# Gate reads a group ahead, four U tiles before the first V product, and the low part of g behind that of V, in a decoder layer's PEER experts

## The chip, the cores and the metric

The kernel runs on one core of a Trainium2 chip. The metric is device time of one launch in microseconds, the median of the runs shown. Five engines work side by side and meet at semaphores: PE (matmuls), DVE (vector), ACT (scalar), POOL (GpSimd, here the row gathers) and SP, which issues loads and stores. All transfers go through 16 DMA engines.

## What is computed

One decoder layer, 512 tokens of width 1024: two token mixers and an output projection, then a PEER layer, which is what the change is about. Each token picks 8 x 16 of 16384 experts by product keys. An expert is a row u and a row v of 1024 numbers:

```python
def peer_ffn(h, w_q, sub_keys, u_tab, v_tab):
    ...
    top_s, pos = lax.top_k(cand, PEER_TOPK)
    e_idx = jnp.take_along_axis(cand_idx, pos, axis=-1)
    gw = jax.nn.softmax(top_s, axis=-1).astype(h.dtype)
    ...
    ue = u_tab[ec]
    ve = v_tab[ec]
    act = jax.nn.gelu(jnp.einsum('td,thkd->thk', hc, ue), approximate=False)
    return jnp.einsum('thk,thkd->td', gc * act, ve)
```

## The kernel before

The kernel computes PEER for the first 384 tokens (TD) densely, without gathers: over all 16384 experts, in 128 tiles of 128 experts. For each tile there is a U product (rows of u times h, then gelu, called act) and a V product, which adds g = gate x act, times rows of v, into six accumulators va. The gate matrix is zero where a token did not pick an expert. It is built while the U tiles run (`w_chunk`, `w_mm`), 24 chunks of 16 tokens, each written to the scratch tensor `wd` in memory by an ACT-issued store. The last 128 tokens go another way: POOL gathers the 256 rows of u and v that each of them picked (`ldg`, one column of indices at a time), and DVE multiplies and adds them (`gather_step`, lines 1171 and 1179).

Numbers are split into a high and a low part for the matmuls: ACT casts the high one (`uhi`, `vhi`, `gshi`, line 122), DVE subtracts to get the low one (`ulo`, `vlo`, `gslo`, line 114). So a U tile is 24 matmuls of 384 columns (lines 1070 to 1072) and a V product is 18 of 512 (lines 1295 to 1297).

There are three stretches. First the loop with `work(...)`: 88 U tiles beside the building of the gate matrix and the first 60 gather steps. The first 8 activations stay on chip (`RING`), the other 80 are spilled to `spill`. Then the V loop: for each of the first 40 products one of the 40 U tiles that are left runs too, with about three gather steps. Then V alone, 88 products, with about one gather step each. `order` says which tile a product takes: 0 to 7, then the tiles whose activation was never spilled, then the spilled ones from 8 on.

`v_prep(n)` readies product n: it loads the gate group of 8 tiles (`wt`, 1.57 MB in pieces of 512 bytes, two buffers), for spilled tiles a group of 4 activations (`sp`, 0.79 MB, two buffers), and the rows of V (`ld`, 0.52 MB; four buffers, shared with the rows of U). It then makes g, its split and that of V. `vhi` and `vlo` have two buffers, so ACT may cast V of product n only when PE is through with n - 2. DVE's order is that of the code; the order on PE, ACT and SP is made by a scheduler when the program is built. The part of `v_prep` that matters:

```python
        g = vp.tile([P, TD], F32, name="g", bufs=2)
        tt(g.rearrange("p (c t) -> p c t", t=16), wt[:, :, i % 8, :], ac.rearrange("p (c t) -> p c t", t=16), mult)
        gs = split(vp, vp, g, [P, TD], "gs", bufs=KL)
        ...
            v = split(vp, vp, vst[n], [P, D], "v", bufs=2)
```

Of the kernel before, what the change touches and what calls it, by code (L numbers as in the profile page):

```python
# [9 lines left out]
F32 = mybir.dt.float32  # L10
# [10 lines left out]
P = 128  # L21
# [8 lines left out]
TD = 384  # L30
# [78 lines left out]
def layer(ctx: ExitStack, tc: tile.TileContext, a, out):  # L109
    nc = tc.nc  # L110
    mult, add, sub = ALU.mult, ALU.add, ALU.subtract

    def tt(o, i0, i1, op):
        return nc.vector.tensor_tensor(out=o, in0=i0, in1=i1, op=op)  # L114

    def act(o, i, f, **k):
        return nc.scalar.activation(o, i, f, **k)  # L117

    def split(pool_hi, pool_lo, src, shape, tag, bufs=1):
        hi = pool_hi.tile(shape, F32R, name=tag + "hi", bufs=bufs)  # L120
        lo = pool_lo.tile(shape, F32R, name=tag + "lo", bufs=bufs)
        nc.scalar.copy(hi, src)  # L122
        tt(lo, src, hi.bitcast(F32), sub)
        return hi, lo
# [4 lines left out]
    wd = dram.tile([P, TD // 16, NTILE, 16], F32, name="wd")  # L129
# [15 lines left out]
    with ExitStack() as pre:  # L145
# [630 lines left out]
        for i in range(N + 2):  # L776
            n, pr = i // 4, i % 4
# [57 lines left out]
        rt = ctx.enter_context(ExitStack())  # L835
# [212 lines left out]
    spill = dram.tile([P, NTILE, TD], F32, name="spill")  # L1048
    RING = 8

    def ld():
        return ua.tile([P, D], F32, name="ld", bufs=4)

    ust, usp, ue, PU, UB = [], [], [], 2, 3

    def u_split(i):
        if i >= NTILE or i < len(usp):
            return
        while len(ust) < min(i + PU + 1, NTILE):
            ust.append(ld())  # L1060
            nc.sync.dma_start(ust[-1], a["uT"][len(ust) - 1].rearrange("p d e -> p (d e)"))
        src = ust[i].rearrange("p (d e) -> p d e", d=ND)
        usp.append(split(ua, ua, src, [P, ND, P], "u", bufs=UB))

    def u_mm(i, spilled=False):
        u_split(i)
        hi, lo = usp[i]
        ps = psU.tile([P, TD], F32, name="u")
        for d in range(ND):
            nc.tensor.matmul(ps, hi[:, d, :], h2hi[:, d, :TD], start=d == 0, stop=False)  # L1070
            nc.tensor.matmul(ps, hi[:, d, :], h2lo[:, d, :TD], start=False, stop=False)  # L1071
            nc.tensor.matmul(ps, lo[:, d, :], h2hi[:, d, :TD], start=False, stop=d == ND - 1)  # L1072
        ue.append((i, ps, spilled))

    def u_evac():
        if not ue:
            return
        i, ps, spilled = ue.pop(0)
        if spilled:
            ac = up_.tile([P, TD], F32, name="actw", bufs=2)  # L1080
            act(ac, ps, AF.Gelu)
            nc.scalar.dma_start(spill[:, i, :], ac)
        else:
            ac = up_.tile([P, TD], F32, name="act", bufs=RING)
            act(ac, ps, AF.Gelu)
            acts[i] = ac
# [23 lines left out]
    pend = []  # L1110
# [71 lines left out]
    items = [(c, f, 0.0) for c, f in dq]  # L1182
# [10 lines left out]
    r, bud, lead, GR, gcr = 0, 0.0, 3.7, 0.75, 0.0  # L1193

    def work(lim):
        nonlocal bud
        while items and bud > lim:
            c, f, p = items.pop(0)
            f()
            bud += p - c  # L1200

    for i in range(UB - 1):
        u_split(i)
    while items or pend or r % 8:
        bud += lead - 1.14
        todo, pend[:] = list(pend), []
        work(2.0)
        u_split(r + UB - 1)
        u_evac()
        work(0.0)  # L1210
        if gather_on:
            gcr += GR
            while gcr >= 1.0:
                gcr -= 1.0
                gq.pop(0)()
                bud -= 1.2
        for f in todo:
            f()
        u_mm(r, r >= RING)
        r += 1  # L1220
    u_evac()
    rt.close()
    order = list(range(min(RING, r))) + list(range(r, NTILE)) + list(range(RING, r))

    vp = ctx.enter_context(tc.tile_pool(name="vpool", bufs=1, side="left"))
    psV = ctx.enter_context(tc.tile_pool(name="psV", bufs=1, space=PSUM))
    vac = [[psV.tile([P, 512], F32, name=f"va{t}{k}") for k in range(2)] for t in range(ND_T)]
    xos = {}
# [20 lines left out]
            x1_load(t)  # L1249
        final(ND_T)  # L1250

    wts, sps, vst = {}, {}, []
    KL = 4

    vsp = {}

    def v_prep(n):
        if n >= NTILE:
            return
        i = order[n]  # L1260
        if i // 8 not in wts:
            wts.clear()
            wts[i // 8] = vp.tile([P, TD // 16, 8, 16], F32, name="wt", bufs=2)
            nc.sync.dma_start(wts[i // 8], wd[:, :, i // 8 * 8:i // 8 * 8 + 8, :])
        wt = wts[i // 8]
        if i in acts:
            ac = acts.pop(i)
        else:
            if i // 4 not in sps:
                sps.clear()  # L1270
                sps[i // 4] = vp.tile([P, 4, TD], F32, name="sp", bufs=2)
                nc.sync.dma_start(sps[i // 4], spill[:, i // 4 * 4:i // 4 * 4 + 4, :])
            ac = sps[i // 4][:, i % 4, :]
        while len(vst) < min(n + 2, NTILE):
            m = order[len(vst)]
            vst.append(ld())
            nc.sync.dma_start(vst[-1], a["vn"][m * P:(m + 1) * P, :])
        g = vp.tile([P, TD], F32, name="g", bufs=2)
        tt(g.rearrange("p (c t) -> p c t", t=16), wt[:, :, i % 8, :], ac.rearrange("p (c t) -> p c t", t=16), mult)
        gs = split(vp, vp, g, [P, TD], "gs", bufs=KL)  # L1280
        if n >= NTILE - KL + 2:
            v = split(ua, ua, vst[n].rearrange("p (d e) -> p d e", d=ND), [P, ND, P], "u", bufs=UB)
            v = tuple(z.rearrange("p d e -> p (d e)") for z in v)
        else:
            v = split(vp, vp, vst[n], [P, D], "v", bufs=2)
        vsp[n] = gs + v

    def v_mm(n, ts=range(ND_T), kk=range(2)):
# [13 lines left out]
    rho = (sum(base) + 1.46 * len(gq)) / (0.98 * 3.9 * (NTILE + nu))  # L1302
    dma_t, pe_t, nxt = 0.0, 0.0, r
    v_prep(0)
    for n in range(NTILE - KL):
        v_prep(n + 1)
        if nxt < NTILE:
            u_split(nxt + UB - 1)
            u_mm(nxt)
            nxt += 1  # L1310
            pe_t += 3.9
        dma_t += base[n]
        while todo and dma_t < rho * pe_t:
            c, f = todo.pop(0)
            f()
            dma_t += c
        v_mm(n)
        u_evac()
        pe_t += 3.9
    for n in range(NTILE - KL, NTILE):  # L1320
        v_prep(n + 1)
# [27 lines left out]
```

## Time and profile before

| what | value |
|---|---|
| runs | 1631.23, 1631.67, 1636.91 us; median 1631.67 |
| the profiled execution | 1632.98 us, its span 1631.2 us |
| busy: PE, PE's weight loads, DVE, ACT, POOL | 96%, 84%, 80%, 46%, 20% of the span |
| moved by DMA | 413.16 MB |
| V products and the gathers beside them, 915 to 1598 us | DMA engines 0.94 to 0.96 busy, 326 to 338 GB/s |

Busy time of PE is not PE at its peak, since matmuls are pipelined: a matmul is shown as busy from its issue to its end, and the next one begins before that. Where PE is held up must be read from the starts of its matmuls. In a timeline, the number in brackets at a row's end is the time for which the engine stood idle before it, and who ended that wait.

### The profile page before, as it was taken

To read this page: it belongs to the slowest core of one execution; us is meant where nothing else is said; L and a number is where in the kernel's file an instruction comes from. 1 tells how busy PE (TensorE), PEld (TensorE's weight loads), DVE (VectorE), ACT (ScalarE), POOL (GpSimd) and SP (SyncE) were. 2 spreads that over 40 slices of the span, in tenths; PEclk is the share of its full clock that TensorE was granted. 3 is DMA by queue.
4 is the path that set the end of the run, shared out by engine and by line. 5 is a ranking of instruction groups with operands and counts; after the bars stand their busy time and mean duration, and the time that the engine had idled before them with its cause. 6 is when DMAs were issued, how large, how long until landed. Compare 5 with 4: busy or idle time off the path is not lost.

```text
span 1631.2 us, 24125 instructions
## 1 busy us (share of the span) xinstructions
PE 1564.7 (96%) x9033; PEld 1362.5 (84%) x9033; DVE 1297.7 (80%) x2590; ACT 757.8 (46%) x1234; POOL 330.9 (20%) x266
## 2 busy tenths in 40 slices
PE   6999998999999999999999799999999999999998
PEld 3779766898889999999999699998988777877877
DVE  4698667578989999988888587787878777777777
ACT  4345568634335544877877323332332333333332
POOL 0000000000002232222222153454444312222210
PEclk9999999999999999999999899999999999999999
DMA  8443332334016787988888998999999999999993
GB/s 308 154 156 118 116 143 78 120 139 156 1 39 240 260 275 255 324 312 317 311 313 292 310 350 315 334 331 322 333 323 344 315 310 319 347 355 327 326 319 125
DMA packets 153358, 413.16 MB, mean 253 GB/s; under 512 B 12940, under 2 KB 72588, under 8 KB 144152
## 3 DMA queue, kind: packets, MB, share of 16 engines
q1 hardware_dynamic: 100816, 234.37, 41.8%
q0 software_dynamic: 36864, 134.23, 23.1%
q10 hardware_dynamic: 15560, 43.01, 7.0%
q8 instruction: 71, 1.16, 0.3%
q14 instruction: 47, 0.39, 0.1%
HBM read 365.89 MB, written 45.09 MB: 252 GB/s over the span
## 4 chain that ended last, share of the span: by engine, by line
PE 65%; DVE 15%; DMA 13%; ACT 4%; issue 2%; SPq 0%; ACTq 0%; DVEq 0%
DMA ld<-in_vn_dram 9%; PE u L1070 7%; PE u L1071 7%; PE u L1072 7%; PE va L1296 6%; PE va L1297 5%; PE va L1295 5%; DVE ldg L1171 3%; DVE acc L1179 3%; DVE ulo L114 2%; DVE vlo L114 2%; ACT vhi L122 2%; PE mm L1026 2%; PE mm L1025 2%; PE mm L1027 2%
## 5 line engine op out<-in xcount | busy, mean ns | idle before, releaser
L1070 PE MATMUL u<-h2hi,uhi 128*128 128x384 f32 x1024 | 350.8, 343 | 4.2 <-ACT act L117 3.9
L1072 PE MATMUL u<-h2hi,ulo 128*128 128x384 f32 x1024 | 346.8, 339 | 4.3 <-DVE ulo L114 4.3
L1071 PE MATMUL u<-h2lo,uhi 128*128 128x384 f32 x1024 | 348.8, 341 | 0.0
L1163 POOL DMA_INDIRECT ldg<-in_un_dram,e_i x128 | 163.6, 1278 | 884.4 <-DVE cand L114 505.5
L1295 PE MATMUL va<-vhi,gshi 128*128 128x512 f32 x756 | 295.3, 393 | 16.9 <-ACT gshi L122 15.2
L1296 PE MATMUL va<-vlo,gshi 128*128 128x512 f32 x756 | 298.2, 394 | 8.0 <-DVE vlo L114 7.9
L1297 PE MATMUL va<-vhi,gslo 128*128 128x512 f32 x756 | 296.4, 392 | 0.0
L1163 POOL DMA_INDIRECT ldg<-in_vn_dram,e_i x128 | 165.1, 1290 | 350.8 <-DVE acc L1179 311.6
L122 ACT CAST vhi<-ld 128x1024 fp32r<-128x1024 f32 x126 | 132.3, 1051 | 204.6 <-PE va L1297 87.7
L1070 PEld LDWEIGHTS u<-h2hi,uhi 128*128 128x128 f32 x1024 | 194.6, 190 | 7.3 <-ACT act L117 5.1
L122 ACT CAST uhi<-ld 128x1024 fp32r<-128x1024 f32 x130 | 137.6, 1059 | 131.4 <-PE u L1071 75.8
L1072 PEld LDWEIGHTS u<-h2hi,ulo 128*128 128x128 f32 x1024 | 194.3, 190 | 5.0 <-DVE ulo L114 4.9
L1071 PEld LDWEIGHTS u<-h2lo,uhi 128*128 128x128 f32 x1024 | 194.7, 190 | 1.4
L1295 PEld LDWEIGHTS va<-vhi,gshi 128*128 128x128 f32 x756 | 142.8, 189 | 48.9 <-ACT gshi L122 17.5
L1296 PEld LDWEIGHTS va<-vlo,gshi 128*128 128x128 f32 x756 | 142.7, 189 | 41.7 <-DVE vlo L114 13.4
L114 DVE TENSOR_TENSOR ulo<-ld,uhi 128x1024 fp32r<-128x1024 f32 x130 | 158.5, 1220 | 17.6 <-ACT uhi L122 16.1
L114 DVE TENSOR_TENSOR vlo<-ld,vhi 128x1024 fp32r<-128x1024 f32 x126 | 153.8, 1221 | 22.7 <-ACT vhi L122 22.7
L114 DVE TENSOR_TENSOR gslo<-g,gshi 128x384 fp32r<-128x384 f32 x128 | 71.5, 559 | 121.3 <-ACT gshi L122 121.3
L1297 PEld LDWEIGHTS va<-vhi,gslo 128*128 128x128 f32 x756 | 142.7, 189 | 29.3
L1179 DVE SCALAR_TENSOR_TENSOR acc<-ldg,actg,acc 128x1024 f32<-128x1024 f32 x127 | 162.5, 1280 | 0.0
L122 ACT CAST gshi<-g 128x384 fp32r<-128x384 f32 x128 | 65.3, 510 | 196.6 <-DVE g L114 196.3
L1171 DVE SCALAR_TENSOR_TENSOR ldg<-ldg,h2n 128x1024 f32<-128x1024 f32 x128 | 155.9, 1218 | 0.0
(317 smaller groups left out, 2533.1 us busy)
## 6 DMA issues: line engine op xcount, KB each, us to landing
ld<-in_uT_dram SPq DMA_DIRECT2D x128, 512.0 KB
ld<-in_vn_dram SPq DMA_DIRECT2D x128, 512.0 KB
wst<-in_wada_dram SPq DMA_DIRECT2D x24, 1024.0 KB
wd<-wb ACTq DMA_DIRECT2D x24, 1024.0 KB
wt<-wd SPq DMA_DIRECT2D x16, 1536.0 KB
spill<-actw ACTq DMA_DIRECT2D x80, 192.0 KB
sp<-spill SPq DMA_DIRECT2D x20, 768.0 KB
wst<-in_win_dram SPq DMA_DIRECT2D x9, 1024.0 KB
```

The lines of the kernel that those rows point to most:

```text
L114: return nc.vector.tensor_tensor(out=o, in0=i0, in1=i1, op=op)
L122: nc.scalar.copy(hi, src)
L1025: nc.tensor.matmul(ps2[c][:, ms_], hi[:, d, wc], h2hi[:, d, ms_], start=d == 0, stop=False)
L1070: nc.tensor.matmul(ps, hi[:, d, :], h2hi[:, d, :TD], start=d == 0, stop=False)
L1071: nc.tensor.matmul(ps, hi[:, d, :], h2lo[:, d, :TD], start=False, stop=False)
L1072: nc.tensor.matmul(ps, lo[:, d, :], h2hi[:, d, :TD], start=False, stop=d == ND - 1)
L1163: nc.gpsimd.indirect_dma_start(out=gst[-1], out_offset=None, in_=a["un" if kind == "u" else "vn"], in_offset=bass.IndirectOffsetOnAxis(ap= ...
L1171: nc.vector.scalar_tensor_tensor(g, g, 1.0, h2n, op0=mult, op1=mult, accum_out=actg[:, k:k + 1])
L1179: nc.vector.scalar_tensor_tensor(acc, g, actg[:, k:k + 1], acc, op0=mult, op1=add)
L1295: nc.tensor.matmul(vac[t][k], ghi[:, ts_], vhi[:, ks], start=f, stop=False)
L1296: nc.tensor.matmul(vac[t][k], ghi[:, ts_], vlo[:, ks], start=False, stop=False)
L1297: nc.tensor.matmul(vac[t][k], glo[:, ts_], vhi[:, ks], start=False, stop=l)
```

## The change

There are three edits and one that follows from them. The first loop no longer runs on to a multiple of 8 tiles; a second loop runs four more U tiles (and on to a multiple of 4) without gather steps, asks for the first gate group in it, and spills these tiles too. That makes 92 tiles ahead of the V loop, 84 of them spilled. `group_load` keeps the last two groups; `v_prep` asks for the next gate group when it is at the third or seventh tile of a group of 8, and for the next spilled group when it is at the first of a group of 4 and the next one is no more than 12 products away. And the split of g stands behind that of V.

```diff
-    while items or pend or r % 8:
+    while items or pend:
...
+    rt.close()
+
+    vp = ctx.enter_context(tc.tile_pool(name="vpool", bufs=1, side="left"))
+    wts, sps, vst = {}, {}, []
+
+    def group_load(held, k, name, src):
+        if k not in held:
+            held[k] = vp.tile(list(src.shape), F32, name=name, bufs=2)
+            nc.sync.dma_start(held[k], src)
+            for j in list(held)[:-2]:
+                del held[j]
+
+    def w_load(k):
+        group_load(wts, k, "wt", wd[:, :, k * 8:k * 8 + 8, :])
+
+    def s_load(k):
+        group_load(sps, k, "sp", spill[:, k * 4:k * 4 + 4, :])
+
+    last_r = r + 4
+    while r < last_r or r % 4:
+        u_split(r + UB - 1)
+        if r == last_r - 4 + 1:
+            w_load(0)
+        u_evac()
+        u_mm(r, r >= RING)
+        r += 1
     u_evac()
-    rt.close()
...
+    def follow(ks):
+        out = [k for k, j in zip(ks, [None] + ks[:-1]) if k != j]
+        return out
+
+    wseq = follow([i // 8 for i in order])
+    sseq = follow([i // 4 for i in order if RING <= i < r])
...
     def v_prep(n):
...
-        if i // 8 not in wts:
-            wts.clear()
-            wts[i // 8] = vp.tile([P, TD // 16, 8, 16], F32, name="wt", bufs=2)
-            nc.sync.dma_start(wts[i // 8], wd[:, :, i // 8 * 8:i // 8 * 8 + 8, :])
+        if n == 0 or i // 8 != order[n - 1] // 8:
+            w_load(i // 8)
+            wseq.pop(0)
...
-            if i // 4 not in sps:
-                sps.clear()
-                sps[i // 4] = vp.tile([P, 4, TD], F32, name="sp", bufs=2)
-                nc.sync.dma_start(sps[i // 4], spill[:, i // 4 * 4:i // 4 * 4 + 4, :])
+            if i % 4 == 0:
+                s_load(i // 4)
+                sseq.pop(0)
...
+        if i % 4 == 2 and wseq:
+            w_load(wseq[0])
+        if i % 4 == 0 and sseq and n + 12 >= order.index(sseq[0] * 4):
+            s_load(sseq[0])
         g = vp.tile([P, TD], F32, name="g", bufs=2)
         tt(g.rearrange("p (c t) -> p c t", t=16), wt[:, :, i % 8, :], ac.rearrange("p (c t) -> p c t", t=16), mult)
-        gs = split(vp, vp, g, [P, TD], "gs", bufs=KL)
...
             v = split(vp, vp, vst[n], [P, D], "v", bufs=2)
+        gs = split(vp, vp, g, [P, TD], "gs", bufs=KL)
```

SP's order where the first loop ends, before (`ld<-in_uT` and `ld<-in_vn` are rows of U and V, `wt` is a gate group, `sp` a spilled group):

```order
L1061 DMA ld<-in_uT_dram 128x1024 x86
L1277 DMA ld<-in_vn_dram 128x1024 x2
L1264 DMA wt<-wd 128x24x128 x2
L1277 DMA ld<-in_vn_dram 128x1024
L1272 DMA sp<-spill 128x1536
```

and in the changed kernel:

```order
L1061 DMA ld<-in_uT_dram 128x1024 x89
L1229 DMA wt<-wd 128x24x128
L1061 DMA ld<-in_uT_dram 128x1024
L1304 DMA ld<-in_vn_dram 128x1024
L1229 DMA wt<-wd 128x24x128
L1304 DMA ld<-in_vn_dram 128x1024 x2
L1229 DMA sp<-spill 128x1536 x2
```

The two loads of V rows that stood ahead of the first gate group stand behind it now, the second of them behind the second gate group too, and the last U load as well.

DVE's order in one round while U and V alternate, before:

```order
L114 TENSOR_TENSOR g<-wt,act 128x384
L114 TENSOR_TENSOR gslo<-g,gshi 128x384
L114 TENSOR_TENSOR vlo<-ld,vhi 128x1024
L114 TENSOR_TENSOR ulo<-ld,uhi 128x1024
L1171 SCALAR_TENSOR_TENSOR ldg,actg<-ldg,h2n 128x1024
```

and in the changed kernel:

```order
L114 TENSOR_TENSOR g<-wt,act 128x384
L114 TENSOR_TENSOR vlo<-ld,vhi 128x1024
L114 TENSOR_TENSOR gslo<-g,gshi 128x384
L114 TENSOR_TENSOR ulo<-ld,uhi 128x1024
L1171 SCALAR_TENSOR_TENSOR ldg,actg<-ldg,h2n 128x1024
```

Only the low parts of g and V have changed places; on ACT the cast of g still stands ahead of that of V in most of these rounds.

SP's order where V stands alone, before:

```order
L1277 DMA ld<-in_vn_dram 128x1024 x4
L1272 DMA sp<-spill 128x1536
L1277 DMA ld<-in_vn_dram 128x1024 x4
L1272 DMA sp<-spill 128x1536
L1264 DMA wt<-wd 128x24x128
L1277 DMA ld<-in_vn_dram 128x1024 x4
```

and in the changed kernel:

```order
L1304 DMA ld<-in_vn_dram 128x1024 x4
L1229 DMA sp<-spill 128x1536
L1304 DMA ld<-in_vn_dram 128x1024 x4
L1229 DMA sp<-spill 128x1536
L1304 DMA ld<-in_vn_dram 128x1024
L1229 DMA wt<-wd 128x24x128
L1304 DMA ld<-in_vn_dram 128x1024 x3
```

A load of V rows now stands between the spilled group and the gate group at every one of these places; before, it did at two of eight.

## Rows read from the trace of the kernel before

**Rows 1.** PE's timeline: start us, us, engine, line, operation [idle before <-releaser]

```profile
899.84 0.34 PE L1072 MATMUL u<-h2hi,ulo 128*128 128x384 f32 x1
904.00 0.34 PE L1072 MATMUL u<-h2hi,ulo 128*128 128x384 f32 x1
915.49 0.79 PE L1295 MATMUL va<-vhi,gshi 128*128 128x512 f32 x1 [11.15 <-ACT gshi L122]
919.99 0.40 PE L1295 MATMUL va<-vhi,gshi 128*128 128x512 f32 x1
...
924.09 0.39 PE L1295 MATMUL va<-vhi,gshi 128*128 128x512 f32 x1
...
1275.31 0.39 PE L1295 MATMUL va<-vhi,gshi 128*128 128x512 f32 x1
...
1597.06 0.39 PE L1295 MATMUL va<-vhi,gshi 128*128 128x512 f32 x1
...
1626.17 0.39 PE L1297 MATMUL va<-uhi,gslo 128*128 128x512 f32 x1
```

**Rows 2.** SP's and DVE's timelines at the start of V, and a window (PEclk, DMA share, GB/s last)

```profile
904.77 3.85 SPq L1264 DMA_DIRECT2D wt<-wd  x2
914.33 0.56 DVE L114 TENSOR_TENSOR g<-wt,act 128x384 f32<-128x384 f32 x1 [18.64 <-DMA wt<-wd]
922.00:928.00 6.00, 6.00 (x31) 5.38 (x31) 5.42 (x8) 3.29 (x4) 1.49 (x2) 1.00 0.98 380
```

**Rows 3.** DVE's round while U and V alternate, and ACT's cast of V in it

```profile
1104.68 0.55 DVE L114 TENSOR_TENSOR g<-wt,act 128x384 f32<-128x384 f32 x1
1105.82 0.56 DVE L114 TENSOR_TENSOR gslo<-g,gshi 128x384 fp32r<-128x384 f32 x1 [0.58 <-ACT gshi L122]
1106.77 1.23 DVE L114 TENSOR_TENSOR vlo<-ld,vhi 128x1024 fp32r<-128x1024 f32 x1 [0.39 <-ACT vhi L122]
1107.91 1.22 DVE L114 TENSOR_TENSOR ulo<-ld,uhi 128x1024 fp32r<-128x1024 f32 x1
...
1112.58 0.58 DVE L114 TENSOR_TENSOR g<-wt,act 128x384 f32<-128x384 f32 x1
...
1105.69 1.04 ACT L122 CAST vhi<-ld 128x1024 fp32r<-128x1024 f32 x1
```

**Rows 4.** A gate load while U and V alternate: SP, ACT, DVE, PE

```profile
1097.41 0.53 SPq L1264 DMA_DIRECT2D wt<-wd  x1
1117.40 1.04 ACT L122 CAST uhi<-ld 128x1024 fp32r<-128x1024 f32 x1 [10.66 <-DMA ld<-in_uT_dram]
1119.27 0.56 DVE L114 TENSOR_TENSOR gslo<-g,gshi 128x384 fp32r<-128x384 f32 x1 [6.10 <-ACT gshi L122]
1118.88 0.45 PE L1070 MATMUL u<-h2hi,uhi 128*128 128x384 f32 x1 [2.22 <-ACT act L117]
```

**Rows 5.** Gate loads where V stands alone: SP, then PE

```profile
1312.06 0.33 SPq L1272 DMA_DIRECT2D sp<-spill  x1
1312.43 0.53 SPq L1264 DMA_DIRECT2D wt<-wd  x1
...
1384.60 0.33 SPq L1277 DMA_DIRECT2D ld<-in_vn_dram  x1
1384.98 0.64 SPq L1264 DMA_DIRECT2D wt<-wd  x1
...
1332.27 0.50 PE L1295 MATMUL va<-vhi,gshi 128*128 128x512 f32 x1 [0.85 <-ACT gshi L122]
1333.99 0.50 PE L1296 MATMUL va<-vlo,gshi 128*128 128x512 f32 x1 [1.22 <-DVE vlo L114]
```

**Rows 6.** Waits of PE over the whole span: us in total, times, longest

```profile
PE va L1296 <- DVE vlo L114: 7.9, 8, 1.2
```

**Rows 7.** Windows: us, PE, PEld, DVE, ACT, POOL busy, PEclk, DMA share, GB/s

```profile
1272.00:1598.00 326.00, 314.62 (x1371) 256.19 (x1370) 250.91 (x332) 114.76 (x155) 69.42 (x67) 1.00 0.95 326
1372.00:1462.00 90.00, 90.00 (x397) 74.10 (x396) 72.69 (x99) 33.28 (x45) 20.95 (x20) 1.00 0.96 333
```

More of the change, by code (lines that the diff above doesn't have):

```diff
@@ L1220, in layer @@
         r += 1
+    rt.close()
[19 more added lines that the diff above has]
+        r += 1
     u_evac()
-    rt.close()
     order = list(range(min(RING, r))) + list(range(r, NTILE)) + list(range(RING, r))
-    vp = ctx.enter_context(tc.tile_pool(name="vpool", bufs=1, side="left"))
+    def follow(ks):
[3 more added lines that the diff above has]
+    sseq = follow([i // 4 for i in order if RING <= i < r])
     psV = ctx.enter_context(tc.tile_pool(name="psV", bufs=1, space=PSUM))
@@ L1250, in last @@
         final(ND_T)
-    wts, sps, vst = {}, {}, []
     KL = 4
```

## The prediction

> **What bounds the kernel now.** I read first the windows of 40 us, then TensorE's timeline, then what its waits name, and last the rows of SP, ACT and DVE at those waits. TensorE (PE) is at work nearly all the time, and nothing changes before the last U tile of the gather loop ends, at 904.3 [rows 1]. From there to the last V product at 1626.6 lie 722.2 us. One U tile is 24 matmuls, 899.84 to 904.00, so 4.16 us; one V product is 18 matmuls, 919.99 to 924.09, so 4.10 us [rows 1]. Two U tiles already stand ahead of V there, so 38 are left: 38 x 4.16 + 128 x 4.10 = 682.9 us of work. The other 39.3 us are lost, and the change is about these.
>
> They lie in three places. (a) At the start PE stands still for 11.15 us until the gate matrix has come; the load is asked for at 904.77, and DVE's first g waits for it until 914.33 [rows 1, 2]. The first matmuls after it take 0.79 us instead of 0.39 [rows 1]; together about 12.9. (b) From there to 1275.31 (the 47th product) about 11.3 are lost: while U and V alternate, a gate load holds up the loads queued behind it on SP [rows 4], and at the end of the U tiles DVE is behind. (c) From 1275.31 to 1597.06 stand 75 products, 307.5 us of work in 321.75, so 14.3 are lost [rows 1]. About 0.8 remain in the tail.
>
> **Part 1, four U tiles ahead of the first product.** The order on PE has three more U tiles before the first product (93, not 90). They cost nothing, being only moved: 904.3 + 12.5 = 916.8. The gate load can't be asked for earlier than now: it reads what the last write of the gate matrix has stored, and that wait on SP ended at 904.77, so it lands at 914.3 again. But SP now has a U load and then the first V rows behind it, where before the rows had been asked for ahead. These two carry 1.05 MB; at the 380 GB/s of the full queue [rows 2] they come 2.8 us after the gate load's packets, the rows at about 916.3. Cast and subtraction add 1.1 and 1.1 [rows 3], so the first product starts at 918.5. Lost: 1.7 in place of 12.9. Both ends: 0 if the rows come with the gate load, 6 if the second gate load, next on the queue, gets in between and the slow matmuls come back. By the same steps the lower half of the fourth product's rows is ready at 936.4, and PE wants it at 918.5 + 3 x 8.26 = 943.3: a lead of 7 us.
>
> **Part 2, low part of g behind that of V.** While U and V alternate, one round of DVE takes 7.90 us (1104.68 to 1112.58): g, low g, low V, low U, and three gather steps [rows 3]. PE needs 8.26. DVE waits for ACT twice: low g for the cast of g, low V for the cast of V, which on ACT stands behind that of g and ends 2.1 us after g began. Low g lay in that wait, so it was free. Behind low V it is not: the round becomes 7.90 + 0.5 = 8.4. ACT's order is the same as before in 26 of the 32 rounds from the fifth product to the last U tile; in six the cast of V comes first, and there low V follows g at once, 1.5 less, 6.9. So a change that shortens DVE's round where V stands alone takes away its spare time where U and V alternate. The sum from 936.4: 26 x 8.4 + 6 x 6.9 = 259.8; three rounds with a fourth gather step, 3 x 1.2 = 3.5; then two rounds without low U, 2 x 7.2 = 14.4, and one with two steps and V first, 4.5. That is 282.2 to the 39th product.
>
> To this come the gate loads, four in this stretch. Each moves 1.57 MB through SP's queue, and the U load behind it lands so late that ACT, which works in order, stands 10.66 us; DVE's low g then waits 6.10 us where 0.58 is usual, and PE 2.22 [rows 4]. SP's order shows them at the same places relative to the products that use them: each waits, as before, until the last g of an older group has freed its buffer. "A group ahead" is so before already, since there are two buffers. I take 5 us a load on DVE's chain (5.5 in the row, less the half that the longer round gives back), 20 in all; ends 0, if the lead and the v-first rounds swallow them, and 6.4. So the 39th product starts at 936.4 + 282.2 + 20 - 0.3 = 1238.3. PE's own work to there is 38 U tiles and 38 products, 313.9, which is 1218.2. Lost: 20.1, the start included. Before it was 24.2 to the same state of things, so here little is won.
>
> **Part 3, V alone.** Low V is now ready 1.0 us earlier, as low g and its wait are gone from ahead of it; and DVE's round grows shorter by as much. That removes the second gap at each gate load (1333.99, 1.22 us; eight such, 7.9 us in all [rows 5, 6]). The first gap (1332.27, 0.85 [rows 5]) is V rows that come late behind a spilled load and a gate load asked for back to back (1312.06, 1312.43). Where one load of V rows stands between the two, as at 1384.60, no gap follows: PE is busy all 90 us from 1372 to 1462 [rows 5, 7]. The new order has this form at every gate load. I take 5 lost here in place of 14.3 (ends 1 and 14.3), and 1.5 for the gate load that falls just after the last U tile.
>
> **Part 4, what is added.** Four more tiles are spilled: 0.79 MB written and one more load of 0.79 MB. Tiles 88 to 91 now share their gate group with 92 to 95, which come 100 products earlier, so that group is read twice: 17 gate loads for 16, 1.57 MB. They lie near the end, with the loads of x1, when the gathers are through; I take 1.2 more lost in the tail (0 to 6). On ACT four evacuations store instead of keep, which nothing waits for.
>
> **The sum.** 20.1 + 1.5 + 5 + 2.0 = 28.6 lost after, 39.3 before: 10.7 gained. The profiled execution took 1632.98 with a span of 1631.2; against the median of 1631.67 this makes 1621.0.
>
> **Rivals.** *The gate loads stay hidden* (B). The lead of 7 us at the fourth product and the six short rounds take up most of each delay. Against it: a round of 8.4 against PE's 8.26 wins nothing back, so a lead once used up is gone. Then the 39th product comes at 1218.6, lost are 2 + 1.5 + 5 + 2, and the time is 1603.
>
> *The stall only moves* (C). The second gate load comes between and the start loses 5 rather than 1.7; every gate load costs its full 6.4. That is 3.3 + 5.6 more: 1630, no change.
>
> *The DMA engines run full in V alone* (D, slower). One product needs rows 0.524, a share of a gate load 0.197, of a spilled load 0.197 and nearly one gather 0.517, so 1.435 MB, a little more than before as the gathers are spread over fewer U tiles. PE's 4.10 us then ask for 350 GB/s; the stretch ran at 326 with the engines 0.95 busy [rows 7]. If they give no more, a product takes 4.40 us, and 83 of them lose 25 instead of 5: 1641. It decides from 350 GB/s down. Against it: 380 GB/s from 922 to 928, and 90 us without a gap at 0.96 [rows 2, 7]. The Trainium skill ("DMA: Bandwidth & Descriptors", section "Issuing engines are not separate DMA queues") says that transfers from all queues interleave on the same 16 engines, so asking earlier adds no bandwidth, which speaks for this case. Its section "Where 436 GB/s comes from" puts HBM's share of one core at about 358 GB/s; an estimate by it is 4.01 us a product, so PE would stay the bound and the sum 1621, while the 326 of the row makes it 1641. The row of 380 GB/s is above that figure.
>
> **How the numbers follow.** The forecast, 1621, holds 0.55 by itself, from 1612 to 1630; B 0.17, C 0.18, D 0.10. A measurement tells 0.5% from no change, so faster is below 1623.5 and slower above 1639.8. B and some two thirds of the forecast's own range lie below: 0.54; C and the rest between: 0.38; D, mostly, above: 0.08. The range of 8 in 10 takes in C and the half of B in which the loads are hidden in part, and leaves out D and the other half, 0.18: 1605 to 1634.
>
> **What would show it.** PE's gap before the first product should be near 2 us, with the gate load's issue still near 904.8. DVE's round between two g should be about 8.4 with low V waiting for ACT, and 6.9 where V's cast stands first; the gate loads should still show ACT's wait for a U load near 10 us, with PE waiting for ACT or DVE once at most of them. In V alone the gaps before the second matmul of a product should be gone, and those before the first rare. If PE alternates U and V at 8.26 without gaps, B is right; if gaps in V alone come at every product and the engines stay at 0.95 or more, D. The forecast fails most easily in the 20 us of the gate loads.

## The result, and the profile after

| kernel | median (runs) | profiled execution: span |
|---|---|---|
| before | 1631.45 us (1630.84 to 1636.91) | 1631.2 us |
| after | 1614.93 us (1613.07 to 1615.61) | 1613.2 us |

The ratio after / before is 0.989, with a 95% interval from 0.9867 to 0.9912. The change makes the kernel 1.1% faster; 1621.0 was forecast, in a range from 1605 to 1634.

PE's timeline of the changed kernel (start us, us, engine, line, operation, [idle before <-releaser]); the rows that answer to [rows 1] and to the PE row of [rows 4]. Lines 1326 to 1328 are now the V product.

```profile
919.25 0.79 PE L1326 MATMUL va<-vhi,gshi 128*128 128x512 f32 x1 [3.35 <-ACT gshi L122]
...
930.49 0.39 PE L1326 MATMUL va<-vhi,gshi 128*128 128x512 f32 x1
...
1097.95 0.69 PE L1070 MATMUL u<-h2hi,uhi 128*128 128x384 f32 x1 [5.35 <-ACT act L117]
...
1233.43 0.49 PE L1326 MATMUL va<-vhi,gshi 128*128 128x512 f32 x1 [1.51 <-ACT vhi L122]
1234.68 0.50 PE L1327 MATMUL va<-vlo,gshi 128*128 128x512 f32 x1 [0.76 <-DVE vlo L114]
...
1281.33 0.39 PE L1326 MATMUL va<-vhi,gshi 128*128 128x512 f32 x1
...
1587.33 0.39 PE L1326 MATMUL va<-vhi,gshi 128*128 128x512 f32 x1
```

The gap ahead of the first product fell from 11.15 us to 3.35. The last two rows are the 49th and the 124th product: 75 products in 306.00 us, 4.08 each. That is also the shortest spacing of two products in any kernel here, so nothing at all is lost where V stands alone. Before, 75 products there took 321.75 [rows 1].

Windows of the changed kernel (us, PE, PEld, DVE, ACT, POOL busy, PEclk, DMA share, GB/s); the first answers to [rows 7]:

```profile
1290.00:1580.00 290.00, 290.00 (x1281) 240.15 (x1280) 236.37 (x313) 104.63 (x145) 65.97 (x65) 1.00 1.00 353
906.00:916.00 10.00, 9.90 (x58) 9.58 (x56) 1.78 (x2) 1.70 (x3) 0.00 (x0) 1.00 0.97 309
916.00:922.00 6.00, 2.69 (x5) 1.73 (x6) 2.16 (x3) 3.78 (x6) 0.00 (x0) 0.67 1.16 318
922.00:928.00 6.00, 6.00 (x24) 5.11 (x23) 2.72 (x3) 2.96 (x4) 0.00 (x0) 0.77 1.02 391
```

PE is busy for all 290 us of the first window, with the DMA engines at 1.00 and 353 GB/s. The other three are the start of V, and are used below.

SP, ACT and DVE of the changed kernel: the start ([rows 2]), a round while U and V alternate ([rows 3]), a gate load in that stretch ([rows 4]) and one where V stands alone ([rows 5]):

```profile
904.62 0.62 SPq L1229 DMA_DIRECT2D wt<-wd  x1
905.36 3.58 SPq L1061 DMA_DIRECT2D ld<-in_uT_dram  x1
909.06 0.66 SPq L1304 DMA_DIRECT2D ld<-in_vn_dram  x1
915.10 0.56 DVE L114 TENSOR_TENSOR g<-wt,act 128x384 f32<-128x384 f32 x1 [5.35 <-DMA spill<-actw]
917.74 1.04 ACT L122 CAST vhi<-ld 128x1024 fp32r<-128x1024 f32 x1 [8.86 <-DMA ld<-in_vn_dram]
...
1106.35 0.56 DVE L114 TENSOR_TENSOR g<-wt,act 128x384 f32<-128x384 f32 x1
1108.44 1.23 DVE L114 TENSOR_TENSOR vlo<-ld,vhi 128x1024 fp32r<-128x1024 f32 x1 [1.53 <-ACT vhi L122]
...
1114.72 0.58 DVE L114 TENSOR_TENSOR g<-wt,act 128x384 f32<-128x384 f32 x1
...
1076.85 0.53 SPq L1229 DMA_DIRECT2D wt<-wd  x1
1077.99 10.69 SPq L1061 DMA_DIRECT2D ld<-in_uT_dram  x1
1096.46 1.04 ACT L122 CAST uhi<-ld 128x1024 fp32r<-128x1024 f32 x1 [11.44 <-DMA ld<-in_uT_dram]
1100.12 1.23 DVE L114 TENSOR_TENSOR vlo<-ld,vhi 128x1024 fp32r<-128x1024 f32 x1 [8.20 <-ACT vhi L122]
...
1322.77 0.33 SPq L1229 DMA_DIRECT2D sp<-spill  x1
1324.72 0.33 SPq L1304 DMA_DIRECT2D ld<-in_vn_dram  x1
1325.09 0.53 SPq L1229 DMA_DIRECT2D wt<-wd  x1
1328.80 8.49 SPq L1304 DMA_DIRECT2D ld<-in_vn_dram  x3
```

The wait of low V on the cast of V (1.53 us) and the gate load's hold on the U load behind it (11.44 us on ACT) are there as forecast; SP now asks for V rows between the spilled group and the gate group.

**Where the time went.** I count from the end of the 90th U tile and take off the work, 4.16 us a U tile and 4.08 a V product (the spacing just read). Up to the 49th product 38 U tiles and 48 V products are then due in every kernel of this study, 353.9 us; from there to the 124th product 75, which is 306.0. What lies above that is lost. In the kernel before 25.5 us are lost up to the 49th product and 15.5 from there to the 124th (the prediction has 14.3 for V alone, since it counts 4.10 us a product); in the changed kernel 24.1 and 0.0. So 15.5 of the 18.0 us between the two spans were won where V stands alone, and 1.4 in the stretch for which the cover was written. The 90th U tile also ended 1.0 us earlier in this execution, which is no work of the change, and the tail gives 0.2.

The 24.1 of the changed kernel are in four parts, read from the starts of products: 6.3 at the start; 8.7 at two of the four gate loads; 6.7 at the end of the U tiles, from the 36th to the 39th product (the rows at 1233.43 and 1234.68 are of these), where no U tile stands between two V products any more and PE waits for ACT and DVE; and 2.4 spread over the rounds, since U and V in turn take 8.31 us, a little more than 4.16 and 4.08.

The same two numbers for every kernel below, one profiled execution each (the expectations say 48th where the 49th is meant; what is lost between these two is under 0.3 us everywhere). The median of the kernel before lay between 1631 and 1636 us on the chips that ran them, so the ratios are to be compared. From the execution of one kernel to that of the next, the first loss varies by some 5 us, as the changed kernel and the one without requests show, whose orders on SP are the same up to the loads at the end. A difference of less than that in the column of the first loss says nothing.

| kernel | median us | ratio to before, 95% | lost to the 49th | 49th to 124th |
|---|---|---|---|---|
| before | 1631.45 | 1 | 25.5 | 15.5 |
| after | 1614.93 | 0.989 (0.9867, 0.9912) | 24.1 | 0.0 |
| before, order of the low parts alone | 1617.2 | 0.9901 (0.9872, 0.993) | 24.1 | 1.8 |
| after, old order of the low parts | 1635.2 | 1.0022 (0.9988, 1.0057) | 25.7 | 26.8 |
| after, no requests ahead | 1614.5 | 0.9903 (0.9872, 0.9934) | 29.6 | 1.0 |
| after, no cover | 1616.88 | 0.9909 (0.988, 0.9938) | 21.9 | 2.2 |
| order alone, gate load beside the spilled one | 1633.02 | 0.9999 (0.998, 1.0017) | 28.9 | 15.4 |
| before, gate loads on ACT's queue | 1607.6 | 0.9835 (0.9779, 0.9891) | 15.8 | 0.5 |
| after, gate loads on ACT's queue | 1601.05 | 0.982 (0.979, 0.9851) | 9.2 | 0.8 |
| after, a gather ahead of low V | 1601.21 | 0.9838 (0.9784, 0.9892) | 9.6 | 1.1 |
| after, cover of 8 | 1608.94 | 0.9869 (0.9838, 0.99) | 14.6 | 1.4 |
| ACT's queue, rows first | 1602.27 | 0.9798 (0.9743, 0.9853) | 13.5 | 1.6 |
| the same, old order | 1600.43 | 0.9785 (0.9729, 0.9841) | 8.1 | 0.6 |
| ACT's queue, rows first, gather ahead | 1598.45 | 0.9801 (0.9762, 0.984) | 5.1 | 2.2 |

### The profile page after: what moved, and what is told of

The parts are those of the page before. It is cut to its first block, busy times and chain, and to the rows that moved or that the text cites. A ratio compares the mean times of both kernels' runs of the same rounds, so it can differ in the third digit from the quotient of the medians.

```text
span 1613.2 us, 24117 instructions
## 1 busy us (share of the span) xinstructions
PE 1560.4 (97%) x9033; PEld 1361.8 (84%) x9033; DVE 1293.1 (80%) x2590; ACT 755.2 (47%) x1234; POOL 323.3 (20%) x266
## 4 chain that ended last, share of the span: by engine, by line
PE 71%; DVE 16%; DMA 6%; ACT 4%; issue 3%; SPq 0%; ACTq 0%; DVEq 0%
PE va L1327 8%; PE va L1328 8%; PE va L1326 8%; PE u L1070 7%; PE u L1071 7%; PE u L1072 7%; DVE acc L1179 3%; DVE ulo L114 3%; DVE ldg L1171 3%; DMA ld<-in_uT_dram 3%; DMA ld<-in_vn_dram 2%; ACT vhi L122 2%; PE mm L1026 2%; PE mm L1025 2%; PE mm L1027 2%
## 5 line engine op out<-in xcount | busy, mean ns | idle before, releaser
L1163 POOL DMA_INDIRECT ldg<-in_un_dram,e_i x128 | 159.8, 1248 | 869.4 <-DVE cand L114 504.6
L1163 POOL DMA_INDIRECT ldg<-in_vn_dram,e_i x128 | 161.3, 1260 | 362.8 <-DVE acc L1179 321.6
L117 ACT ACTIVATE wb<-mm 128x512 f32<-128x512 f32 x96 | 96.1, 1110 | 47.2 <-PE mm L1134 47.1
```

Of the source, the lines that this page charges most:

```text
L1163: nc.gpsimd.indirect_dma_start(out=gst[-1], out_offset=None, in_=a["un" if kind == "u" else "vn"], in_offset=bass.IndirectOffsetOnAxis(ap= ...
```

## Experiments: which part of the change pays

**The order of the low parts alone**, put into the kernel before:

```diff
-        gs = split(vp, vp, g, [P, TD], "gs", bufs=KL)
...
             v = split(vp, vp, vst[n], [P, D], "v", bufs=2)
+        gs = split(vp, vp, g, [P, TD], "gs", bufs=KL)
```

> The kernel before with one edit: the low part of g stands behind that of V. Theory P (each part of the change acts in its own place): the order alone empties V alone, where before lost 14.3 us (the row of 8 waits for vlo, 7.9 us, goes, and the scheduler puts V rows between the spilled load and the gate load at every place); the gap of 11.15 us before the first product stays; while U and V alternate the round grows from 7.90 to 8.4 and that stretch loses 11 to 15 in place of 11.3. Time 1617 to 1621, 11 to 14 below before. Rival R (the requests a group ahead empty V alone): V alone still loses 10 or more here, 1627 to 1633.

Measured: 0.9901 of before, the gain of the whole change within the interval. In V alone 1.8 us are lost in place of 15.5. The requests ahead don't carry V alone; rival R falls.

**The changed kernel with the old order** (the same diff, reversed):

> The changed kernel with the split of g put back ahead of that of V; cover and requests stay. Theory P: waits for vlo in V alone come back, 10 to 14 us lost there where the changed kernel loses 0; while U and V alternate the shorter round of 7.9 wins back after each gate load, so of the 15.4 us that the changed kernel loses from its second to its 39th product 3 to 6 are saved; start as in the changed kernel. Time 1621 to 1626. Rival R: V alone stays without gaps, and with the shorter rounds the time is 1609 to 1613, below the changed kernel.

Measured: 1.0022, no gain at all, and above the range of either theory. Cover and requests alone give nothing. V alone lost 26.8 us, more than the 14 that P took, but the profiled execution was a long one, 1643.65 us against a median of 1635.2. What the shorter round should have saved before V alone did not show (25.7 against 24.1).

**No requests ahead**, which takes these lines out:

```diff
-        if i % 4 == 2 and wseq:
-            w_load(wseq[0])
-        if i % 4 == 0 and sseq and n + 12 >= order.index(sseq[0] * 4):
-            s_load(sseq[0])
```

> The changed kernel without the two requests of the next gate and spilled group in v_prep, so that a group is asked for where it is first used. Theory P: a load waits for its buffer in either form, and the order on SP is the same up to the loads at the very end, so the time stays within 2 us of the changed kernel's 1614.9. Rival R: V alone loses 10 or more again, 1625 or more.

Measured: 0.9903, the same as the changed kernel, with SP's order the same up to the loads of x1 at the end. The requests do nothing: a load goes out when its buffer is free, and with two buffers that is a group ahead in either form.

**No cover** (the second loop taken out, `r % 8` back in the first):

> The changed kernel without its second loop: 88 tiles ahead of V, the first gate group asked for in the first v_prep; requests and order stay. Theory P: PE stands about 11 us before its first product again and loses 12.9 at the start where the changed kernel loses 6.2, the 17th gate load and four spilled tiles go, and all else stays: 1619 to 1623, and the same as the kernel with the order alone within 2 us. Rival Q (the cover only moves the wait, by a later gate load or by the extra loads): 1613 to 1616, the same as the changed kernel.

Measured: 0.9909. PE stands 11.06 us ahead of the first product again, and yet the loss up to the 49th product is 21.9, not the 31 that P asked for. By its time, 1616.88, it lies 1 us above Q's range and 2 below P's, and by the loss up to the 49th product Q is right: what the cover wins at the start it gives back before the U tiles end. What the runs say on how stands with the gather experiment and the cover of eight tiles below.

## Experiments: why the order empties V alone

The order does two things. It makes low V ready a microsecond earlier, and it changes what the scheduler does on SP: of the eight gate loads in V alone, two had V rows between the spilled load and the gate load before, and all do now. This experiment keeps the first and undoes the second. The gate load is put beside the spilled load by a higher priority for both. It then stands just ahead of the spilled load and not just behind it, and at all eight places, where in the kernel before the two stood together at six:

```diff
-            nc.sync.dma_start(wts[i // 8], wd[:, :, i // 8 * 8:i // 8 * 8 + 8, :])
+            with tc.high_priority() if n >= 44 else ExitStack():
+                nc.sync.dma_start(wts[i // 8], wd[:, :, i // 8 * 8:i // 8 * 8 + 8, :])
...
-                nc.sync.dma_start(sps[i // 4], spill[:, i // 4 * 4:i // 4 * 4 + 4, :])
+                with tc.high_priority() if n >= 44 else ExitStack():
+                    nc.sync.dma_start(sps[i // 4], spill[:, i // 4 * 4:i // 4 * 4 + 4, :])
```

> The kernel before with low g behind low V, and the gate load put directly beside the spilled load on SP where V stands alone, with no V rows between. Theory S (low V ready a microsecond earlier is what empties V alone): at most 3 us of gaps there, and the time is that of the order alone, 1615 to 1620 beside 1634 for the kernel before. Rival T (it is the V rows that the scheduler now puts between the two loads): 1 to 2.5 us lost again at each of the eight places, 8 to 20 in all, 1625 to 1637.

Measured: 0.9999, no gain, with 15.4 us lost in V alone. Theory S falls. SP, ACT and PE of this kernel at one of the gate loads, in order of time, and the window (columns as above) just behind it:

```profile
1311.03 0.53 SPq L1265 DMA_DIRECT2D wt<-wd  x1
1311.61 8.78 SPq L1274 DMA_DIRECT2D sp<-spill  x1
1320.49 5.06 SPq L1279 DMA_DIRECT2D ld<-in_vn_dram  x4
1331.14 1.04 ACT L122 CAST vhi<-ld 128x1024 fp32r<-128x1024 f32 x1 [6.80 <-DMA ld<-in_vn_dram]
1332.65 0.49 PE L1297 MATMUL va<-vhi,gshi 128*128 128x512 f32 x1 [1.69 <-ACT gshi L122]
1333.49 0.49 PE L1298 MATMUL va<-vlo,gshi 128*128 128x512 f32 x1 [0.35 <-DVE vlo L114]
1334.56 0.63 PE L1297 MATMUL va<-vhi,gshi 128*128 128x512 f32 x1
...
1332.00:1338.00 6.00, 5.00 (x13) 3.62 (x14) 4.26 (x6) 2.05 (x4) 0.00 (x0) 0.72 0.78 308
```

and SP of the kernel with the order alone, where rows stand between the two:

```profile
1339.13 0.33 SPq L1272 DMA_DIRECT2D sp<-spill  x1
1341.13 0.33 SPq L1277 DMA_DIRECT2D ld<-in_vn_dram  x1
1341.51 1.21 SPq L1264 DMA_DIRECT2D wt<-wd  x1
1345.21 8.88 SPq L1277 DMA_DIRECT2D ld<-in_vn_dram  x3
```

SP is stuck 8.78 us in asking for the second of two large loads, the next V rows are asked for at 1320.49, and ACT stands 6.80 us for rows. The early low V did what the prediction said: the gap before the second matmul shrank from 1.22 to 0.35. But the one before the first grew from 0.85 to 1.69 [rows 5]. The delay sits in the rows; which matmul shows it depends on DVE's order.

That 15.4 us are lost here and 15.5 before does not make the early low V worth nothing. PE's gaps in V alone add up to 6.2 us here and to 11.4 before; the rest is lost behind the gaps. At this place and at two others the granted clock fell to the lower level for a while (PEclk 0.72 in the window shown, 0.63 us a matmul in place of 0.39), where V alone of the kernel before ran at 1.00 [rows 7]. And by places, two loads together cost some 1.9 us here (eight) and 2.6 before (six). By this count the early low V saves some 0.7 us at a place where the rows come late, and the rows between save the larger part; the two loads also stand in the other order here, and no run separates that.

The kernel with the old order says the same from the other side. At the five places where its two loads stand together it loses 1.9, 1.3, 1.0, 4.4 and 4.8 us (gaps alone, read some 20 us behind each gate load), at the three with rows between 0, 0.8 and 1.5. So the rows between count most, without being all of it there. No run has rows between at every place together with the old order.

**The gate loads on another queue.** If it is the rows behind the gate load on SP, the order should not matter once that load is asked for elsewhere. In the kernel before, with nothing else changed:

```diff
-    wts, sps, vst = {}, {}, []
+    wts, sps, vst, wn = {}, {}, [], []
...
-            nc.sync.dma_start(wts[i // 8], wd[:, :, i // 8 * 8:i // 8 * 8 + 8, :])
+            wn.append(i)
+            (nc.scalar if len(wn) > 2 else nc.sync).dma_start(wts[i // 8], wd[:, :, i // 8 * 8:i // 8 * 8 + 8, :])
```

> The kernel before with one edit: its gate loads from the third on are asked for on ACT's queue; low g stays ahead of low V, no cover, no requests. Theory Q (a gate load costs time only by the rows that queue behind it on SP): V alone loses 0 to 2 in place of 14.3 and the stretch with U tiles 0 to 4 in place of 11.3, the start keeps its 12.9: 1606 to 1613. Rival O (the order of the low parts is needed besides): 5 or more stay lost in V alone, 1614 to 1622.

Measured: 0.9835, its median in Q's range, and at least as good as the whole change, from one edited load. ACT and SP of this kernel, and its window in V alone:

```profile
1330.55 0.33 SPq L1273 DMA_DIRECT2D sp<-spill  x1
1330.56 0.53 ACTq L1265 DMA_DIRECT2D wt<-wd  x1
1333.06 8.63 SPq L1278 DMA_DIRECT2D ld<-in_vn_dram  x3
```

```profile
1290.00:1580.00 290.00, 289.89 (x1278) 239.11 (x1277) 233.08 (x309) 106.78 (x146) 60.43 (x59) 1.00 0.94 336
```

Here the two large loads go out within 0.01 us of each other, and together at all eight places, with the old order of the low parts, and PE loses 0.5 us in 75 products. Theory Q holds. The bytes are the same as before (413.16 MB); only the queue is another.

The same edit in the changed kernel:

> The changed kernel with all gate loads but the first two asked for on ACT's queue, so that no load of U or V rows stands behind one on SP's. Theory Q (a gate load costs time because the row loads queue behind its 3072 pieces): ACT no longer stands 11 us for a U load at the 21st round, the 8.7 us that the changed kernel loses at gate loads while U and V alternate go, and the time is 1604 to 1609. Rival E (the 1.57 MB themselves delay the rows, whatever queue carries them, since the engines are nearly full): 5 or more of the 8.7 stay, 1611 to 1617.

Measured: 0.982, below Q's range. ACT, SP's next load of U rows, and the window while U and V alternate:

```profile
1073.17 0.53 ACTq L1229 DMA_DIRECT2D wt<-wd  x1
1074.29 0.33 SPq L1061 DMA_DIRECT2D ld<-in_uT_dram  x1
1085.80 1.05 ACT L122 CAST uhi<-ld 128x1024 fp32r<-128x1024 f32 x1 [4.48 <-DMA ld<-in_uT_dram]
```

```profile
1100.00:1200.00 100.00, 100.00 (x507) 91.04 (x507) 84.68 (x106) 33.99 (x48) 47.70 (x37) 1.00 0.95 348
```

ACT's wait for the U load is 4.48 us in place of 11.44, and PE loses nothing at the four gate loads: all its rounds from the second to the 36th product take 8.31. Rival E falls. SP asks for the next U rows in 0.33 us; in the changed kernel, behind the gate load, that took it 10.69 (the row at 1077.99). What is left up to the 49th product is mostly the start.

## Experiments: the start, and the stretch where U and V alternate

To see why the cover's gain is given back I take the lead: PE's start of a product less the end of its low V on DVE. In the changed kernel it is 9.9 us at the 9th product (the most in any of these kernels, V having two buffers), 5.7 at the 10th, behind a gate load, and 2.4 at the 14th, behind the next. It then falls by 0.05 a round, since DVE's round is 8.37 us (1106.35 to 1114.72) and PE's 8.31. At the 22nd product comes the third load, and PE stops for 5.35 us. In the kernel before, with DVE's round of 7.90, the lead grows by 0.4 a round, from 2.8 to 5.8 between the 10th and the 17th product.

**A gather step into DVE's wait** of 1.53 us, while there are U tiles (`step`, not shown, runs the next gather step if one is due):

```diff
-    def v_prep(n):
+    def v_prep(n, fill=None):
...
         tt(g.rearrange("p (c t) -> p c t", t=16), wt[:, :, i % 8, :], ac.rearrange("p (c t) -> p c t", t=16), mult)
+        if fill:
+            fill()
...
-        v_prep(n + 1)
+        v_prep(n + 1, step if nxt < NTILE else None)
```

> The changed kernel with one gather step per round moved into the 1.53 us in which DVE waits between g and low V, while U and V alternate. Theory D (DVE's round of 8.4 against PE's 8.3 is why a lead once used up is gone, and why PE loses 6.7 at the end of the U tiles): the round falls to about 6.9, the lead is back at its cap of 5.6 us before each gate load, the 8.7 lost at gate loads become 0 to 4 and the 6.7 at the end of the U tiles 2 to 5: 1604 to 1611. Rival G (a gather row comes late and now holds up low V as well): PE waits for vlo at more places, 1615 or more.

Measured: 0.9838. DVE's round in this kernel:

```profile
1113.56 0.55 DVE L114 TENSOR_TENSOR g<-wt,act 128x384 f32<-128x384 f32 x1
1114.03 1.28 DVE L1179 SCALAR_TENSOR_TENSOR acc<-ldg,actg,acc 128x1024 f32<-128x1024 f32 x1
1115.64 1.23 DVE L114 TENSOR_TENSOR vlo<-ld,vhi 128x1024 fp32r<-128x1024 f32 x1 [0.34 <-ACT vhi L122]
...
1120.73 0.56 DVE L114 TENSOR_TENSOR g<-wt,act 128x384 f32<-128x384 f32 x1
```

The round is 7.17, not the 6.9 expected, and 0.34 of waiting stays in it. The lead grows by 1.13 a round, and 9.6 us are lost up to the 49th product in place of 24.1. (The cap of 5.6 us in the expectation is none: the lead reached 9.9 at the 9th and the 29th product.) So theory D holds: with a round longer than PE's, each gate load's delay stays for good. No run has the gather step without the cover, so what the cover would be worth beside the shorter round isn't shown.

**A cover of eight tiles** (`last_r = r + 8`):

> The changed kernel with eight U tiles in the second loop in place of four: 96 tiles ahead of V, so gate groups are read whole and 8 products apart, 16 in all. Theory N (the 4-tile cover is too short for gate load, rows and cast, and its half group puts two gate loads four products apart, which eats the lead): no gap before the first product, 0 to 2 lost at the start in place of 6.2, 0 to 3 at gate loads in place of 8.7, and 4 us given back since gathers move to V alone: 1602 to 1609. Rival M (more gathers in V alone fill the engines): products there take over 4.15 us, 1614 or more.

Measured: 0.9869. Its median is 6 us below that of the changed kernel and at the upper end of N's range, but the ratios differ by 0.002 and their intervals overlap, so the two can't be told apart by time. The start did not empty as N said: PE still stood 1.91 us, since the scheduler put U rows and spilled groups ahead of the first V rows on SP, too. V alone lost 1.4, so rival M falls. N's other half fares better. With gate groups read whole PE lost 1.8 us at the gate loads in place of 8.7, and without any cover nothing. The four-tile cover splits a group, and its first two gate loads while U and V alternate go out 37 us apart (968.34 and 1005.27); without a cover they are 71 apart (957.43 and 1028.27). So the split group is a rival reason for the cover's gain being given back. How much is due to it and how much to DVE's round, no run separates.

**V rows ahead of the first gate load**, with the gate loads on ACT's queue:

```diff
+        if r == last_r - 3:
+            for m in range(1):
+                vst.append(ld())
+                with tc.high_priority(offset=400):
+                    nc.sync.dma_start(vst[-1], a["vn"][m * P:(m + 1) * P, :])
```

> The changed kernel with the gate loads from the third on asked for on ACT's queue, and with the first V rows asked for ahead of the first gate load. Theory N (the first product of the changed kernel waits for V rows that come behind the gate load and a U load, 6.2 us lost with the slow matmuls after it): the gap before the first product goes, 0 to 1 us lost there, and the time is 5 to 6 below that with the gate loads on ACT alone: 1594 to 1597. Rival L (the gate matrix itself comes after the last U tile of the cover): 2 us of gap and the half clock stay, 1599 to 1602.

Measured: 1602.27, no better than without, a miss. PE of this kernel:

```profile
911.86 0.44 PE L1070 MATMUL u<-h2hi,uhi 128*128 128x384 f32 x1 [1.20 <-ACT actw L117]
...
916.14 0.39 PE L1332 MATMUL va<-vhi,gshi 128*128 128x512 f32 x1
```

The first product starts at 916.14, with no gap and at the higher clock (PEclk 1.00 from 916 to 922): N's mechanism is there. But 13.5 us are lost up to the 49th product, where the kernel with a late first product lost 9.2. The 4.3 between them is no more than executions differ by, but the 6 us won at the start are nowhere to be seen. The lead at the 5th product is 5.6 us here and 9.5 there: PE began earlier, DVE did not, and at the 22nd product the lead is gone.

**The same with the old order of the low parts:**

> The kernel of gate loads on ACT and rows first, with the split of g put back ahead of that of V. Theory Q (the order of the low parts pays only because the scheduler then puts V rows between two loads on SP, and with gate loads off that queue it has nothing left to do): within 3 us of the same kernel with the new order. Rival O (low V ready earlier is worth something by itself): 5 us or more slower than that.

Measured: 1600.43, 1.8 us below the new order. Theory Q holds: off SP's queue, the order of the change is worth nothing by itself.

**The same with the gather step ahead of low V:**

> The kernel of gate loads on ACT and rows first, with one gather step per round moved between g and low V while U and V alternate. Theory D (from the fourth product to the last U tile DVE's chain sets the pace, so what PE wins at the start it gives back at the end of the U tiles, 13.5 us lost to the 48th product with an early first product and 9.2 with a late one): with a round of about 6.9 in place of 8.4 the early start is kept, 3 to 6 lost to the 48th product, 1592 to 1597. Rival H (the stores and loads beside the first gate load cost it, or the gathers now bind): 9 or more lost to the 48th product, 1599 or more.

Measured: 5.1 us lost up to the 49th product, in D's range; the lead is 9.9 at nearly every product from the 16th to the 36th. The time, 1598.45, is 1.5 above D's range, since 2.2 us are lost in V alone and PE waits 1.73 us at the 124th product. It has the lowest median, but the kernels at 1598 to 1602 us can't be told apart by their intervals. All of them lie below the changed kernel, and those with gate loads on ACT's queue by their intervals too, against 0.9867 to 0.9912.

## Why the prediction was right, point by point

**V alone: 5 us forecast, nothing measured.** This is the term that was off. The prediction named both effects, low V earlier (7.9 us of second gaps) and rows between the two loads, and put the larger part on the first. The runs put nearly all of it on the rows: with the early low V and no rows between 15.4 us are lost, with rows between 1.8, and with the old order and the gate loads on ACT's queue 0.5. The two places of before that had this form, at 1384.60 [rows 5] and 1520, lost nothing. Taken at their word they said 0, not 5.

**Up to the end of the U tiles: little was to be won, and little was.** The 39th product was forecast at 1238.3; it started at 1240.5. The mechanism was the one forecast: DVE's chain sets that time, and from the low V of the 4th product (ready at 937.6, forecast 936.4) to that of the 39th (1239.0) it took 301.4 us, forecast 301.9. The terms held less well than the sum. At the *start* 6.3 us are lost, not 1.7: the load was asked for at 904.62 and g began at 915.10, near the forecast, but the V rows came 1.4 us later than the step said. It had them move at 380 GB/s; behind the gate load's small pieces the window from 906 to 916 moved 309 at a share of 0.97. And 3.35 us of idle PE brought the slow matmuls back: PEclk is 0.67 and 0.77 in the next two windows, and the first product with its U tile took 11.24 us (919.25 to 930.49) in place of 8.31, 2.9 more. The end of 6 that the prediction kept for this was the right one, but not by the cause that it named: the second gate load stood behind the first V rows. The forecast of the 39th product did not suffer from it, since PE's late start only gave DVE a longer lead (9.5 us at the fourth product, forecast 7).

The *round* of 8.4 was right (8.37), and so was its reason. *The gate loads* were taken at 5 us each on DVE's chain. They took 4.2, 3.0, 6.7 and 4.0 (low V to low V, less the round): 17.9 in place of 20. PE lost 8.7 us at two of them, the lead paid for the other two.

**The gate load just behind the last U tile** cost nothing (1.5 forecast), and the tail 0.7 in place of 2.0: the 17th gate load and the 21st spilled load cost nothing that shows there.

**The requests** were said to change nothing, and change nothing.

**The rivals.** B (loads hidden) was half true: two of four. C (the stall only moves) is what happened to the cover, which the kernel without it shows, though not at C's prices: the start lost more than its 5, and the four gate loads took 17.9 of DVE's chain, not four times 6.4. The forecast had the gain in V alone in spite of it. D (engines full) falls: it asked for less than 350 GB/s, and the stretch ran at 353 with a share of 1.00 and without a gap. The Trainium skill's figure of about 358 GB/s ("DMA: Bandwidth & Descriptors", section "Where 436 GB/s comes from") stands 1.4% above the long window; the 6 us from 922 to 928 show 391, so it is no ceiling for short stretches here.

## What to carry to other kernels

Here a load of 1.57 MB in pieces of 512 bytes delayed what was asked for behind it on its queue (whether by its size or by its pieces was not tried). Look first at what else is queued there, and try the load on another queue, before buying cover for it. When an edit to compute order changes the time, compare the order of the transfers too: here the gain was gone once the place where the scheduler had put a load was undone. And time given to the engine that waits came back as a later wait here, as long as the chain that feeds it had a round longer than its own.

## What was not expected of the hardware

The queue matters at equal bytes. The kernel before and its twin with gate loads on ACT's queue move the same bytes through the same engines at the same placement or a closer one, and the twin is 1.65% faster. The Trainium skill ("DMA: Bandwidth & Descriptors", section "Issuing engines are not separate DMA queues") says that issuing from several engines saves only the time that it takes to issue, usually small beside the transfer. Here that time is not small: behind a gate load on its queue SP took 10.69 us to ask for the next U rows, with the gate load on ACT's queue 0.33, and ACT's wait for these rows was 11.44 us and 4.48. Whether the rows come earlier because SP is free to ask for them, or because they no longer stand behind the gate load's pieces, no run here separates.

A wait of PE can cost more than itself. After 3.35 us of idle time 2.9 more were lost at a PEclk of 0.67 and 0.77, which are means over stretches partly at the lower of the two levels; after 5.35 us (1097.95) the product took 15.9 us in place of 8.3, 2.2 more than the gap. In V alone of the kernel before, waits of up to 1.90 us left the clock at 1.00 and only the first one or two matmuls after them longer, 0.50 us in place of 0.39. In the kernel with the gate load beside the spilled one, waits of 1.69 and 0.35 us in a row were followed by matmuls of 0.63 us, at a PEclk of 0.72 from 1332 to 1338. So from these rows the length of a wait alone does not tell what it costs.
